# A hybrid decoder layer on one core: the attention query projection moved to the front of the input projections, with the scores of two blocks between their pieces

## The chip, the core and the metric

The kernel runs on one core of a Trainium2 chip. The core has five engines that run side by side and meet through semaphores: TensorE (PE, the matmuls; its weight loads are shown as PEld), VectorE (DVE), ScalarE (ACT), GpSimd (POOL) and SyncE (SP, which here only starts DMA transfers; ACT's queue starts some too). The metric is device time in microseconds (us) of one execution.

## The reference

One decoder layer over 512 tokens of width 1024, in float32. Token mixing: a combined input projection feeds four mLSTM heads and eight sliding-window attention heads, and one output projection takes both. Cross-attention into 256 memory tokens and a retrieval over 16384 experts (PEER) follow; the change does not touch them.

```python
y = rmsnorm(x, g_mix) @ w_in          # mLSTM q, k, v, o gate, i and f gates; attention q, k, v
qk = silu(causal_depthwise_conv(q|k))  # width 4
hm = mlstm_chunkwise(q, k, v, i, f)    # decays exp(log f sums + i), carried state per head
hm = rmsnorm per head(hm) * g_mhead * sigmoid(o)
ha = sliding_window_gqa_sinks(aq, ak, av, sinks)   # window 128: a block sees itself and the block before
x = x + concat(hm, ha) @ w_out
x = x + memory_cross_attention(rmsnorm(x), rmsnorm(mem))
x = x + peer_ffn(rmsnorm(x))
```

## The kernel before, in words

All matmuls keep float32 accuracy with three products: an operand is cut into a high and a low part (`whi`, `wlo` for weights, `xhi`, `xlo` for activations; ACT casts, DVE subtracts; `load_w` L985 and `split_psum` L942), and hi x hi, lo x hi, hi x lo accumulate in PSUM. A projection of 512 columns is two halves of the depth, each with four accumulators (`acc_f` with features in the partitions, `acc_t` with tokens): eight pieces of 12 matmuls each. A weight half is one SP transfer, one cast of 2048 columns and one subtraction, or four of each with 512 columns (`parts=4`).

The front stage, `front()`, makes in this order: the norm of x, the mLSTM values, the small projections (attention k and v, gates), the qk projection with convolution and silu (`evac_qk` L197), the output gate's projection mo with its sigmoid into `gm` (`evac_mo` L214), the decay matrices `ab` (L226) and their sixteen exponentials `dt` (L232), then the attention query projection aq (`evac_aq` L384). Between the pieces of aq a scheduler places, by its own costs and due times, the mLSTM heads' products `st` (L241) with `pt = st * dt` (L244), the carry `wb` (L250) and the first two blocks of `mlstm` (L268).

The tokens stand in four blocks of 128. From there on the order of PE is written out by a table, `MIX` (L62), inside `tc.manual_schedule`: a word is a kind and a block, and each takes one step of a generator. `s` is a block's attention (`swa` L318: scores of the first four heads; scores of the last four and the softmax; transposes of the probabilities, once for block 0 and twice for the others; products with the values), `m` is `mlstm` (numerators; then the state), `n` is `mlstm_out` (normalise, gate, transpose, split), `x` is the output projection's half step for a block (`mix0` L396), `w` loads a half of the output weights.

The orders of ACT, DVE and POOL come from the scheduler, which follows the program with priorities. PSUM has eight banks in three groups by tag: `a`, `b` and `d`. In `swa` of before the scores take banks of `b`.

The reload of `h` (x again, for the residual sums), 4 transfers of 512 KB on SP's queue, and the 8 MB zero fill of a buffer in HBM, on ACT's queue, are issued once the aq projection is through.

Of the kernel before, what the change touches and what calls it, by code (L numbers as in the profile page):

```python
# [11 lines left out]
F32 = mybir.dt.float32  # L12
# [4 lines left out]
AF = mybir.ActivationFunctionType  # L17
ALU = mybir.AluOpType
# [14 lines left out]
NK = 128  # L33
# [7 lines left out]
UG = 4  # L41
# [39 lines left out]
def front(c):  # L81

    tc, nc, a = c.tc, c.nc, c.a
    ident, ps = c.ident, c.ps
    fp = c.fp
# [52 lines left out]
    tp = ps.tile([P, 512], F32, tag="a", name="tp_v")  # L138
    for b in range(NB):
        T.transpose(tp[:, b * P:(b + 1) * P], avT[:, b * P:(b + 1) * P], ident)  # L140
    V.tensor_copy(av, tp.rearrange("p (b d) -> p b d", b=NB))


    t0 = c.np_.tile([P, D], F32, tag="xs", bufs=4, name="rowt0")
# [41 lines left out]
    for b in range(NB):  # L186
        tp = ps.tile([P, 512], F32, tag="a", name="tp_r")
        T.transpose(tp[:, :96], rows[0:96, b * P:(b + 1) * P], ident[:96, :96])
        V.tensor_copy(cols[:, b], tp[:, :96])
# [22 lines left out]
    gm = fp.tile([P, NB, 512], F32, name="gm")  # L212
# [8 lines left out]
    pt, dts = [], []  # L221

    abs_ = [ps.tile([P, 512], F32, tag=t_, name="ab") for t_ in "ddaa"]
    for h in range(4):
        r = slice(32 * h, 32 * h + 4)
        T.matmul(abs_[h], c.sel[r, h], raf4[r], start=True, stop=False)  # L226
    for h in range(4):
        T.matmul(abs_[h], c.identb, c.cmask, start=False, stop=True)
    for h in range(4):
        dt = c.np_.tile([P, D], F32, tag="xs", bufs=4, name="dt")[:, :S]  # L230
        for b in range(NB):
            A.activation(dt[:, b * P:(b + 1) * P], abs_[h][:, b * P:(b + 1) * P], AF.Exp, bias=cols[:, b, h:h + 1])  # L232
        dts.append(dt)
    for pr in range(2):
# [12 lines left out]
    wbs = [ps.tile([P, 512], F32, tag="d", name="wb") for _ in range(2)]
    for pr in (1, 0):
        r = slice(32 * pr, 32 * pr + 4)
        T.matmul(wbs[pr], c.selp[r, pr], wi4[r].rearrange("p b t -> p (b t)"), start=True, stop=True)  # L250
    for pr, wb in enumerate(wbs):
        V.tensor_copy(dec[:, pr], wb.rearrange("p (b t) -> p b t", b=NB)[:, :, P - 1])
        V.tensor_tensor(qk[:, pr], wb, qk[:, pr], op=ALU.mult)
# [63 lines left out]
    def swa(b):  # L317
# [7 lines left out]
        mx = fp.tile([P, 8], F32, tag="mx", bufs=2, name="mx")  # L325
        for jj in range(2):

            sps = [ps.tile([P, 512], F32, tag="b", name="sp") for _ in gs]
            for j2 in range(2):
                for g, r in enumerate(gs):  # L330
                    T.matmul(sps[g][:, j2 * 256:j2 * 256 + nk], aq[r, 2 * jj + j2, t], kT[r, k0:k0 + nk],
                             start=True, stop=True)
            for j2 in range(2):
                for g in range(2):
                    h = 4 * g + 2 * jj + j2
                    V.tensor_tensor_reduce(sc[:, h, :nk], sps[g][:, j2 * 256:j2 * 256 + nk], msk, 1.0, FMIN,
                                           op0=ALU.add, op1=ALU.max, accum_out=mx[:, h:h + 1])
            if jj == 0:
                yield
# [38 lines left out]
    ml = [mlstm(b) for b in range(NB)]  # L378
    for b in range(2):
        step(ml[b], 2)  # L380
    aq = fp.tile([P, 4, S], F32, name="aq")

    def evac_aq(j, acc):
        c.act_aq = A.copy(aq[:, j], acc)  # L384

    gemm_fm(c, [a["w_in_m"][3, hf] for hf in range(2)], evac_aq)

    with tc.issue_after(c.raw_dma.ins):
        for b in range(NB):
            nc.sync.dma_start(c.h[:, b], a["x"][:, b])  # L390
    with tc.issue_after(c.act_aq.ins):
        c.zd = nc.scalar.dma_start(c.wd[0].rearrange("g p n -> p g n"),
                                   zero.unsqueeze(1).to_broadcast([P, NK // UG, P * UG]))
    wo = []

    def mix0(b):  # L396
        acc = ps.tile([P, 512], F32, tag="b", name="acc_o")
        for hf in range(2):
            mm3_tm(c, acc, wo[hf], slice(0, 512), hf, b)
            if hf == 0:  # L400
                yield
        resid(c, b, 0, acc)

    it = {"s": [swa(b) for b in range(NB)], "x": [mix0(b) for b in range(NB)], "m": ml}
    with tc.manual_schedule(engines={mybir.EngineType.PE}):
        for op in MIX.split():
            k, b = op[0], int(op[1])
            if k == "n":
                mlstm_out(b)
            elif k == "w":  # L410
                wo.append(load_w(c, a["w_out"][0, b], 512, parts=4, hp=0 if b else HP))
# [878 lines left out]
```

## Time and profile before

| | |
|---|---|
| median of 3 runs | 1652.22 us (1652.19 to 1653.87) |
| profiled execution | 1653.3 us |
| its span, first to last instruction | 1651.5 us |
| PE busy | 1609.7 us (97%) |
| DVE, ACT, POOL busy | 1235.1 (75%), 723.6 (44%), 591.1 us (36%) |
| mean granted TensorE clock | 0.989 |
| chain that ended last | PE 89%, DVE 4%, DMA 3%, ACT 2% |

The profile is of one execution. A busy share is an average over stages with different limits, so a stage is read from its own rows: the timeline lists each instruction with the idle time of its engine before it and what released it; the waits sum that idle time by line; the windows give busy time and the granted clock of a stretch. [...]

### The profile page before, as it was taken

To read this page: it belongs to the slowest core of one execution; us is meant where nothing else is said; L and a number is where in the kernel's file an instruction comes from. 1 tells how busy PE (TensorE), PEld (TensorE's weight loads), DVE (VectorE), ACT (ScalarE), POOL (GpSimd) and SP (SyncE) were. 2 spreads that over 40 slices of the span, in tenths; PEclk is the share of its full clock that TensorE was granted. 3 is DMA by queue.
4 is the path that set the end of the run, shared out by engine and by line. 5 is a ranking of instruction groups with operands and counts; after the bars stand their busy time and mean duration, and the time that the engine had idled before them with its cause. 6 is when DMAs were issued, how large, how long until landed. Compare 5 with 4: busy or idle time off the path is not lost.

```text
span 1651.5 us, 23090 instructions
## 1 busy us (share of the span) xinstructions
PE 1609.7 (97%) x8388; PEld 1415.1 (86%) x8388; DVE 1235.1 (75%) x2704; ACT 723.6 (44%) x1217; POOL 591.1 (36%) x427
## 2 busy tenths in 40 slices
PE   8998899999999999999999999999999999999994
PEld 5776688878999999999998888888888888888883
DVE  5546564464787887777796888788888888888898
ACT  5445544342544454678664333333333333333332
POOL 2000000000027787877221543444433434334451
PEclk9999999999999999999999999999999999999997
DMA  5236134232254435678999999999989889988895
GB/s 214 77 127 255 59 126 173 77 153 106 96 168 145 116 71 141 181 190 213 342 305 339 410 393 347 343 342 338 334 335 367 338 321 333 362 317 320 323 364 181
DMA packets 151122, 402.17 MB, mean 244 GB/s; under 512 B 28368, under 2 KB 62304, under 8 KB 138848
## 3 DMA queue, kind: packets, MB, share of 16 engines
q1 hardware_dynamic: 58208, 240.04, 39.0%
q0 software_dynamic: 55360, 134.32, 24.8%
q10 hardware_dynamic: 37440, 26.35, 5.1%
q8 instruction: 66, 1.08, 0.3%
q14 instruction: 48, 0.39, 0.1%
HBM read 357.07 MB, written 43.58 MB: 243 GB/s over the span
## 4 chain that ended last, share of the span: by engine, by line
PE 89%; DVE 4%; DMA 3%; ACT 2%; issue 1%; POOL 0%; DVEq 0%; SPq 0%; POOLq 0%; ACTq 0%
PE acc_u L907 10%; PE acc_u L908 10%; PE acc_u L909 10%; PE acc_d L836 10%; PE acc_d L834 10%; PE acc_d L835 10%; PE acc_f L1008 4%; PE acc_f L1009 4%; PE acc_f L1010 4%; PE w L740 3%; DMA wd<-stg 3%; PE acc_t L1023 2%; PE acc_t L1022 2%; PE acc_t L1021 2%; DVE gacc L778 1%
## 5 line engine op out<-in xcount | busy, mean ns | idle before, releaser
L834 PE MATMUL acc_d<-xhi,dh 128*128 128x384 f32 x1024 | 349.8, 342 | 1.0 <-ACT gsp L856 1.0
L836 PE MATMUL acc_d<-xhi,dl 128*128 128x384 f32 x1024 | 345.0, 337 | 1.7 <-DVE dl L823 1.7
L835 PE MATMUL acc_d<-xlo,dh 128*128 128x384 f32 x1024 | 343.6, 336 | 0.0
L908 PE MATMUL acc_u<-ul,ch 128*128 128x512 f32 x762 | 297.7, 391 | 0.0
L909 PE MATMUL acc_u<-uh,cl 128*128 128x512 f32 x762 | 296.6, 391 | 0.0
L685 POOL DMA_INDIRECT wd<-gg,ei x128 | 231.6, 1810 | 147.6 <-DVE ei L679 84.8
L907 PE MATMUL acc_u<-uh,ch 128*128 128x512 f32 x762 | 264.4, 390 | 0.2 <-ACT ch L895 0.2
L762 POOL DMA_INDIRECT rows<-in_up_dram,rowid x128 | 169.4, 1323 | 236.8 <-DVE gacc L778 208.9
L823 DVE TENSOR_TENSOR dl<-draw,dh 128x1024 fp32r<-128x1024 f32 x128 | 156.1, 1220 | 92.8 <-ACT dh L785 90.3
L895 ACT CAST ch<-cf 128x384 fp32r<-128x384 f32 x127 | 65.1, 514 | 356.3 <-issue 339.2
L785 ACT CAST dh<-draw 128x1024 fp32r<-128x1024 f32 x128 | 134.0, 1049 | 195.6 <-PE acc_d L835 170.8
L762 POOL DMA_INDIRECT rows<-in_down_r_dram,rowid x106 | 142.6, 1346 | 199.1 <-DVE dots L768 158.4
L834 PEld LDWEIGHTS acc_d<-xhi,dh 128*128 128x128 f32 x1024 | 192.8, 188 | 5.3 <-ACT gsp L856 1.3
L836 PEld LDWEIGHTS acc_d<-xhi,dl 128*128 128x128 f32 x1024 | 192.6, 188 | 3.9 <-DVE dl L823 2.6
L835 PEld LDWEIGHTS acc_d<-xlo,dh 128*128 128x128 f32 x1024 | 192.8, 188 | 3.7
L909 PEld LDWEIGHTS acc_u<-uh,cl 128*128 128x128 f32 x762 | 143.0, 188 | 29.4
L908 PEld LDWEIGHTS acc_u<-ul,ch 128*128 128x128 f32 x762 | 143.0, 188 | 28.7
L907 PEld LDWEIGHTS acc_u<-uh,ch 128*128 128x128 f32 x762 | 142.9, 188 | 28.3 <-ACT ch L895 0.5
L886 DVE TENSOR_TENSOR ul<-uraw,uh 128x1024 fp32r<-128x1024 f32 x127 | 154.8, 1220 | 12.5 <-ACT uh L785 12.3
L778 DVE SCALAR_TENSOR_TENSOR gacc<-rows,coef,gacc 128x1024 f32<-128x1024 f32 x127 | 162.6, 1280 | 0.9
L768 DVE CUSTOM_DVE_ANT_0 rows<-rows,xn 128x1024 f32<-128x1024 f32 x128 | 153.7, 1218 | 0.0
L896 DVE TENSOR_TENSOR cl<-cf,ch 128x384 fp32r<-128x384 f32 x127 | 70.7, 557 | 86.4 <-ACT ch L895 79.9
(344 smaller groups left out, 2654.0 us busy)
## 6 DMA issues: line engine op xcount, KB each, us to landing
draw<-in_down_t_dram SPq DMA_DIRECT2D x64, 1024.0 KB
uraw<-in_up_dram SPq DMA_DIRECT2D x64, 1024.0 KB
wt<-wd SPq DMA_DIRECT2D x96, 256.0 KB
wd<-stg ACTq DMA_DIRECT2D x8, 2048.0 KB
gd<-gsp SPq DMA_DIRECT2D x18, 768.0 KB
gsr<-gd SPq DMA_DIRECT2D x18, 768.0 KB
wd<-zero ACTq DMA_DIRECT2D x1, 8192.0 KB
raw<-in_w_pq_dram SPq DMA_DIRECT2D x8, 1024.0 KB
```

Source lines behind the costliest of these rows:

```text
L685: i = G.indirect_dma_start(out=out, out_offset=bass.IndirectOffsetOnAxis(ap=ei[:, h, k:k + 1], axis=0), in_=c.gg[:, NG, hh, k:k + 1], in_o ...
L762: G.indirect_dma_start(out=r, out_offset=None, in_=src, in_offset=bass.IndirectOffsetOnAxis(ap=c.rowid[:, j:j + 1], axis=0))
L768: V.tensor_tensor_reduce(r, r, c.xn0, 1.0, 0.0, op0=ALU.mult, op1=ALU.add, accum_out=dots[:, j:j + 1])
L778: V.scalar_tensor_tensor(c.gacc, r, coef[:, j:j + 1], c.gacc, op0=ALU.mult, op1=ALU.add)
L823: c.dl = nc.vector.tensor_tensor(self.lo, raw, f32(self.hi), op=ALU.subtract)
L834: T.matmul(acc[:, :TD], self.hi[:, ks], c.xhi[:, k, NG * P:], start=(k == 0), stop=False)
L835: T.matmul(acc[:, :TD], self.hi[:, ks], c.xlo[:, k, NG * P:], start=False, stop=False)
L836: T.matmul(acc[:, :TD], self.lo[:, ks], c.xhi[:, k, NG * P:], start=False, stop=(k == KT - 1))
L886: V.tensor_tensor(lo, raw, f32(hi), op=ALU.subtract)
L907: T.matmul(acc[b][n], ch[:, t], hi[:, d], start=st, stop=False)
L908: T.matmul(acc[b][n], ch[:, t], lo[:, d], start=False, stop=False)
L909: c.mm = T.matmul(acc[b][n], cl[:, t], hi[:, d], start=False, stop=sp)
```

## The change

The aq projection comes first, then qk, then mo, each as a generator of eight pieces, and `MIX` now writes the order of PE from the first of these pieces on. New words: `a`, `q`, `g` (a piece of aq, qk, mo), `t` and `c` (the transposes of the attention values and of the gate columns), `d` (the decays), `e` (a pair of mLSTM heads), `f` (the carry). The scores of blocks 0 and 1 stand between pieces of qk and use PSUM tag `d`; block 0's transposes stand in mo. `rows` moves to another pool, and `gm`, `aq` and `pt` are allocated ahead. The reload of `h` and the zero fill are issued behind the second half of the output weights.

```diff
-MIX = ("w0 s0 s0 n0 n1 s1 m2 s1 x0 m2 s0 w1 x1 s0 m3 x0 s2 s1 s2 s1 s3 n2 s1 n3 s3 x2 x1 s2 s2 s2 x3 s3 x2 s3 s3 x3")
+MIX = ("a0 a0 a0 t0 a0 a0 a0 a0 a0 c0 q0 s0 q0 q0 s0 q0 q0 s1 q0 q0 s1 q0 g0 g0 d0 g0 g0 w0 e0 g0 e1 s0 g0 f0 m0 g0 m0 g0 w1 "
+       "n0 s0 m1 s2 s1 x0 m1 s1 s2 n1 x0 s1 m2 s3 x1 m2 s2 x1 s3 n2 m3 s2 s2 n3 x2 s3 x2 s3 x3 s3 x3")
...
-    rows = f1.tile([P, S], F32, name="rows")
+    rows = c.np_.tile([P, D], F32, tag="xs", bufs=4, name="rows")[:, :S]
...
     fp = c.fs.enter_context(c.pool("front2"))
+    gm = fp.tile([P, NB, 512], F32, name="gm")
+    aq = fp.tile([P, 4, S], F32, name="aq")
     qk = fp.tile([P, 4, S], F32, name="qk")
...
-    gemm_fm(c, [a["w_in_m"][0, hf] for hf in range(2)], evac_qk)
...
     def evac_mo(b, acc):
-        A.activation(gm[:, b], acc, AF.Sigmoid)
+        c.act_mo = A.activation(gm[:, b], acc, AF.Sigmoid)
         V.tensor_tensor(gm[:, b], gm[:, b], c.gmh, op=ALU.mult)
-    gemm_tm(c, [a["w_in_m"][2, hf] for hf in range(2)], evac_mo)
...
-            sps = [ps.tile([P, 512], F32, tag="b", name="sp") for _ in gs]
+            sps = [ps.tile([P, 512], F32, tag="d" if b < 2 else "b", name="sp") for _ in gs]
...
-    for b in range(2):
-        step(ml[b], 2)
...
-    gemm_fm(c, [a["w_in_m"][3, hf] for hf in range(2)], evac_aq)
-
-    with tc.issue_after(c.raw_dma.ins):
-        for b in range(NB):
-            nc.sync.dma_start(c.h[:, b], a["x"][:, b])
-    with tc.issue_after(c.act_aq.ins):
-        c.zd = nc.scalar.dma_start(c.wd[0].rearrange("g p n -> p g n"),
...
-    it = {"s": [swa(b) for b in range(NB)], "x": [mix0(b) for b in range(NB)], "m": ml}
+    it = {"s": [swa(b) for b in range(NB)], "x": [mix0(b) for b in range(NB)], "m": [mlstm(b) for b in range(NB)],
+          "a": [fm_parts(c, [a["w_in_m"][3, hf] for hf in range(2)], evac_aq)],
+          "q": [fm_parts(c, [a["w_in_m"][0, hf] for hf in range(2)], evac_qk)],
+          "g": [tm_parts(c, [a["w_in_m"][2, hf] for hf in range(2)], evac_mo)]}
+    once = {"t": lambda _: tr_v(), "c": lambda _: tr_c(), "d": lambda _: decays(), "e": heads, "f": lambda _: carry(),
+            "n": mlstm_out,
+            "w": lambda h: wo.append(load_w(c, a["w_out"][0, h], 512, parts=4, hp=0 if h else HP))}
...
+            if op == "w1":
+                with tc.issue_after(c.raw_dma.ins):
+                    for b in range(NB):
+                        nc.sync.dma_start(c.h[:, b], a["x"][:, b])
+                with tc.issue_after(c.act_mo.ins):
+                    c.zd = nc.scalar.dma_start(c.wd[0].rearrange("g p n -> p g n"),
...
+def fm_parts(c, src, evac):
+
+    acc = [c.ps.tile([P, 512], F32, tag="b", name=f"acc_f{j}") for j in range(4)]
+    for hf in range(2):
+        w = load_w(c, src[hf], 512)
+        for j in range(4):
+            mm3_fm(c, acc[j], w, j, hf, S)
+            if hf:
+                evac(j, acc[j])
+            yield
```

`tm_parts` is the same with `acc_t` and `mm3_tm`. `tr_v`, `tr_c`, `decays`, `heads` and `carry` hold the old code of these steps. The changed kernel's line numbers differ from those of before; the rows below carry each kernel's own.

ACT before, from the cast of aq's first half (`whi` 128x2048) past the decays; `acc_t` is the mo projection, `gm` its sigmoid:

```order
L995 CAST whi<-raw 128x2048
L215 ACTIVATE gm<-acc_t_685 128x512
L232 ACT_TABLE_LOAD
L232 ACTIVATE dt<-ab,cols 128x128 x16
L995 CAST whi<-raw 128x512 x4
L384 COPY aq<-acc_f_958 128x512
```

ACT in the change, from the last copy of the qk projection (`convraw`) to the cast of mo's second half; `sc` are the scores of block 1, `qk<-convy` is the silu:

```order
L209 COPY convraw<-acc_f_663 128x512
L357 ACT_TABLE_LOAD
L357 ACTIVATE sc,den_863<-sc,nm 128x256
L355 ACTIVATE es<-es 128x8
L357 ACTIVATE sc,den_863<-sc,nm 128x256 x7
L215 ACT_TABLE_LOAD
L215 ACTIVATE qk<-convy 128x512
L363 ACTIVATE sc<-sc,den_863 128x256 x4
L215 ACTIVATE qk<-convy 128x512
L238 ACT_TABLE_LOAD
L238 ACTIVATE dt<-ab,cols 128x128 x16
L1002 CAST whi<-raw 128x2048
```

The exponentials and scalings of block 1 and two silus, with three table loads, now stand ahead of `dt`, and a cast that PE needs stands behind it.

PE before, in the query projection, around the first pair of heads (`st`); `acc_f` is aq:

```order
L1010 MATMUL acc_f_960<-xhi,wlo 128x512
L241 MATMUL st<-qk 128x128 [waits PE_49,Activation_49]
L241 MATMUL st<-qk 128x128 x2
L241 MATMUL st<-qk 128x128 [waits PE_49,Activation_49]
L241 MATMUL st<-qk 128x128 x4
L1008 MATMUL acc_f_960<-xhi,whi 128x512
```

PE in the change, from the end of mo's fourth piece; `acc_t_904` is the first piece of mo's second half:

```order
L1030 MATMUL acc_t_907<-whi,xlo 128x512
L248 MATMUL st<-qk 128x128 [waits DVE_49,PE_49,Activation_49]
L248 MATMUL st<-qk 128x128 [waits PE_49,Activation_49]
L248 MATMUL st<-qk 128x128 x6
L1028 MATMUL acc_t_904<-whi,xhi 128x512 [waits Activation_49]
L1029 MATMUL acc_t_904<-wlo,xhi 128x512 [waits DVE_49]
L1030 MATMUL acc_t_904<-whi,xlo 128x512
```

The heads now stand between two pieces of mo, directly ahead of the first product that needs mo's second weight half; before, they stood inside aq, whose matmuls went on after them.

ACT before, from the squares of block 3 of the mLSTM (`junk_h`) to the exponentials of block 3's softmax (`den_1487`; `den_1399` is block 2's):

```order
L290 ACTIVATE junk_h,hss<-hm 128x128 x4
L366 COPY pT<-tp_p 128x512 x2
L348 ACTIVATE sc,den_1399<-sc,nm 128x256
L346 ACTIVATE es<-es 128x8
L348 ACTIVATE sc,den_1399<-sc,nm 128x256 x7
L942 CAST xhi<-tp_hm 128x4x128
L942 CAST xhi<-o_att 128x4x128
L942 CAST xhi<-tp_hm 128x4x128
L354 ACTIVATE sc<-sc,den_1399 128x256 x4
L348 ACTIVATE sc,den_1487<-sc,nm 128x256
L346 ACTIVATE es<-es 128x8
L348 ACTIVATE sc,den_1487<-sc,nm 128x256 x7
```

ACT in the change, from the softmax of block 3 (`den_1462`) to the split of block 3's mLSTM heads (`tp_hm`):

```order
L357 ACTIVATE sc,den_1462<-sc,nm 128x256
L355 ACTIVATE es<-es 128x8
L357 ACTIVATE sc,den_1462<-sc,nm 128x256 x7
L293 ACTIVATE den<-num 128x2 x2
L375 COPY pT<-tp_p 128x512
L363 ACTIVATE sc<-sc,den_1462 128x256 x4
L949 CAST xhi<-o_att 128x4x128
L299 ACTIVATE junk_h,hss<-hm 128x128 x4
L949 CAST xhi<-tp_hm 128x4x128
```

The squares of block 3 stood ahead of the softmaxes of blocks 2 and 3, with three splits (`xhi`) between the two; now they stand behind block 3's exponentials, a copy, the scalings and a cast, directly ahead of their split.

## Rows read from the trace of the kernel before

**Rows 1.** PE waits, 230 us to the end: engine, line, releaser: us in total, times, longest.
```profile
PE w L740 <- DVE oh L739: 2.0, 1, 2.0
...
PE acc_u L907 <- ACT ch L895: 0.2, 1, 0.2
```

**Rows 2.** Timeline of PE, 136 to 202 us: start, duration, instruction, [idle before].
```profile
139.63 0.96 PE L298 MATMUL ds<-vx,kw 128*64 128x129 f32 x8 [1.65 <-DVE hm L289]
142.85 1.17 PE L312 MATMUL tp_hm<-ident,hm 128*128 128x128 f32 x4 [1.50 <-DVE hm L310]
...
179.25 0.77 PE L1021 MATMUL acc_o<-whi,xhi 128*128 128x512 f32 x1 [3.21 <-DVE mx L336]
189.36 1.09 PE L363 MATMUL tp_p<-ident,sc 128*128 128x128 f32 x8 [0.68 <-ACT pT L366]
```

**Rows 3.** Windows: PE, PEld, DVE, ACT, POOL busy, granted clock, DMA share, GB/s.
```profile
140.00:148.00 8.00, 6.43 (x33) 4.28 (x31) 6.14 (x28) 6.37 (x29) 1.01 (x1) 0.57 1.04 370
178.00:186.00 8.00, 6.75 (x17) 5.36 (x18) 3.76 (x17) 5.58 (x22) 0.00 (x0) 0.57 0.00 0
```

**Rows 4.** Timeline of PE, 55 to 175 us, single rows.
```profile
55.90 0.40 PE L1008 MATMUL acc_f<-xhi,whi 128*128 128x512 f32 x1
56.13 0.40 PE L1009 MATMUL acc_f<-xlo,whi 128*128 128x512 f32 x1
...
103.49 0.59 PE L1008 MATMUL acc_f<-xhi,whi 128*128 128x512 f32 x1
...
119.33 1.17 PE L241 MATMUL st<-qk 64*128 64x128 f32 x16
...
160.51 0.71 PE L277 MATMUL num<-vx,pt 128*128 128x129 f32 x4
162.64 0.50 PE L1021 MATMUL acc_o<-whi,xhi 128*128 128x512 f32 x1
...
165.65 1.14 PE L331 MATMUL sp<-kT,aq 64*128 64x256 f32 x8
166.71 1.09 PE L363 MATMUL tp_p<-ident,sc 128*128 128x128 f32 x8
...
172.44 1.94 PE L373 MATMUL o_att<-pT,av 128*64 128x512 f32 x8
```

**Rows 5.** Timeline of ACT, 79 to 178 us.
```profile
79.36 1.15 ACT L206 ACTIVATE qk<-convy 128x512 f32<-128x512 f32 x2
...
101.88 1.90 ACT L995 CAST whi<-raw 128x2048 fp32r<-128x2048 f32 x1 [2.26 <-PE acc_t L1023]
...
104.29 1.28 ACT L232 ACT_TABLE_LOAD   x1
105.59 4.23 ACT L232 ACTIVATE dt<-ab,cols 128x128 f32<-128x128 f32 x16
118.97 2.18 ACT L995 CAST whi<-raw 128x512 fp32r<-128x512 f32 x4 [9.15 <-PE acc_f L1009]
...
128.19 0.30 ACT L290 ACTIVATE junk_h<-hm 128x128 f32<-128x128 f32 x1
...
133.04 0.39 ACTq L392 DMA_DIRECT2D wd<-zero  x1
...
177.70 1.71 ACT L354 ACTIVATE sc<-sc,den 128x256 f32<-128x256 f32 x4
```

**Rows 6.** Groups of ACT, 40 to 230 us: count, busy us, mean ns, idle before.
```profile
L348 ACT ACTIVATE sc<-sc,nm 128x256 f32<-128x256 f32 x24 | 11.9, 495 | 5.6 <-DVE nm L342 5.6
```

**Rows 7.** Timeline of DVE, 71 to 168 us.
```profile
71.16 2.29 DVE L996 TENSOR_TENSOR wlo<-raw,whi 128x2048 fp32r<-128x2048 f32 x1 [2.82 <-ACT whi L995]
...
131.42 1.14 DVE L310 SCALAR_TENSOR_TENSOR hm<-hm,rst,gm 128x128 f32<-128x128 f32 x4 [1.14 <-POOL rst L938]
...
167.89 0.42 DVE L336 CUSTOM_DVE_ANT_0 sc<-sp,band 128x256 f32<-128x256 f32 x1
```

**Rows 8.** Timeline of SP's queue, 60 to 240 us.
```profile
192.34 0.80 SPq L436 DMA_DIRECT2D mem<-in_mem_dram  x2
```

More of the change, by code (lines that the diff above doesn't have):

```diff
@@ L185, in front, with tr_c @@
     cols = fp.tile([P, NB, 96], F32, name="cols")
[L186 to L189, printed above, removed]
+    def tr_c():
+        for b in range(NB):
+            tp = ps.tile([P, 512], F32, tag="a", name="tp_r")
+            T.transpose(tp[:, :96], rows[0:96, b * P:(b + 1) * P], ident[:96, :96])
+            V.tensor_copy(cols[:, b], tp[:, :96])
     f1s.close()
     fp = c.fs.enter_context(c.pool("front2"))
+    gm = fp.tile([P, NB, 512], F32, name="gm")
+    aq = fp.tile([P, 4, S], F32, name="aq")
     qk = fp.tile([P, 4, S], F32, name="qk")
@@ L208, in evac_qk, with decays, heads @@
             V.tensor_scalar(qk[:, j], qk[:, j], 0.125, None, op0=ALU.mult)
-    gemm_fm(c, [a["w_in_m"][0, hf] for hf in range(2)], evac_qk)
-    gm = fp.tile([P, NB, 512], F32, name="gm")
     def evac_mo(b, acc):
-        A.activation(gm[:, b], acc, AF.Sigmoid)
+        c.act_mo = A.activation(gm[:, b], acc, AF.Sigmoid)
         V.tensor_tensor(gm[:, b], gm[:, b], c.gmh, op=ALU.mult)
-    gemm_tm(c, [a["w_in_m"][2, hf] for hf in range(2)], evac_mo)
[L221 to L234, printed above, removed]
+    pt = [fp.tile([P, S], F32, name=f"pt{h}") for h in range(4)]
+    dts = []
+    def decays():
+        abs_ = [ps.tile([P, 512], F32, tag=t_, name="ab") for t_ in "ddaa"]
+        for h in range(4):
+            r = slice(32 * h, 32 * h + 4)
+            T.matmul(abs_[h], c.sel[r, h], raf4[r], start=True, stop=False)
+        for h in range(4):
+            T.matmul(abs_[h], c.identb, c.cmask, start=False, stop=True)
+        for h in range(4):
+            dt = c.np_.tile([P, D], F32, tag="xs", bufs=4, name="dt")[:, :S]
+            for b in range(NB):
+                A.activation(dt[:, b * P:(b + 1) * P], abs_[h][:, b * P:(b + 1) * P], AF.Exp, bias=cols[:, b, h:h + 1])
+            dts.append(dt)
+    def heads(pr):
         sts = [ps.tile([P, 512], F32, tag="a", name="st") for _ in range(2)]
@@ L242, in front, with carry @@
         for hh in range(2):
-            pth = fp.tile([P, S], F32, name=f"pt{2 * pr + hh}")
-            V.tensor_tensor(pth, sts[hh], dts[2 * pr + hh], op=ALU.mult)
-            pt.append(pth)
+            V.tensor_tensor(pt[2 * pr + hh], sts[hh], dts[2 * pr + hh], op=ALU.mult)
     dec = fp.tile([P, 2, NB], F32, name="dec")
[L247 to L253, printed above, removed]
+    def carry():
+        wbs = [ps.tile([P, 512], F32, tag="d", name="wb") for _ in range(2)]
+        for pr in (1, 0):
+            r = slice(32 * pr, 32 * pr + 4)
+            T.matmul(wbs[pr], c.selp[r, pr], wi4[r].rearrange("p b t -> p (b t)"), start=True, stop=True)
+        for pr, wb in enumerate(wbs):
+            V.tensor_copy(dec[:, pr], wb.rearrange("p (b t) -> p b t", b=NB)[:, :, P - 1])
+            V.tensor_tensor(qk[:, pr], wb, qk[:, pr], op=ALU.mult)
     def make_kw(b):
@@ L376, in swa @@
             split_psum(c, c.xhi[:, 4:8, t], c.xlo[:, 4:8, t], o.rearrange("p (h t) -> p h t", h=4))
-    ml = [mlstm(b) for b in range(NB)]
-    for b in range(2):
-        step(ml[b], 2)
-    aq = fp.tile([P, 4, S], F32, name="aq")
     def evac_aq(j, acc):
-        c.act_aq = A.copy(aq[:, j], acc)
-    gemm_fm(c, [a["w_in_m"][3, hf] for hf in range(2)], evac_aq)
-    with tc.issue_after(c.raw_dma.ins):
-        for b in range(NB):
-            nc.sync.dma_start(c.h[:, b], a["x"][:, b])
-    with tc.issue_after(c.act_aq.ins):
-        c.zd = nc.scalar.dma_start(c.wd[0].rearrange("g p n -> p g n"),
-                                   zero.unsqueeze(1).to_broadcast([P, NK // UG, P * UG]))
+        A.copy(aq[:, j], acc)
     wo = []
@@ L407, in front @@
             k, b = op[0], int(op[1])
[L408 to L411, printed above, removed]
+            if k in once:
+                once[k](b)
             else:
                 step(it[k][b], 1)
+            if op == "w1":
+                with tc.issue_after(c.raw_dma.ins):
+                    for b in range(NB):
+                        nc.sync.dma_start(c.h[:, b], a["x"][:, b])
+                with tc.issue_after(c.act_mo.ins):
+                    c.zd = nc.scalar.dma_start(c.wd[0].rearrange("g p n -> p g n"),
+                                               zero.unsqueeze(1).to_broadcast([P, NK // UG, P * UG]))
     for k in it.values():
@@ L1041, in gemm_fm, with tm_parts @@
                 evac(j, acc[j])
+def fm_parts(c, src, evac):
[7 more added lines that the diff above has]
+            yield
+def tm_parts(c, src, evac):
+    acc = [c.ps.tile([P, 512], F32, tag="b", name=f"acc_t{j}") for j in range(NB)]
+    for hf in range(2):
+        w = load_w(c, src[hf], 512)
+        for b in range(NB):
+            mm3_tm(c, acc[b], w, slice(0, 512), hf, b)
+            if hf:
+                evac(b, acc[b])
+            yield
 def gemm_tm(c, src, evac, parts=1):
```

7 lines of the change are left out of this document (4 added, 3 removed).

## The prediction

> **What bounds the kernel now.** I read the waits of TensorE (PE) first, over the whole span. From 230 us to the end it waits at seven places, 6.9 us together and nowhere longer than 2.0 [rows 1], and the change orders nothing there anew: whatever the front stage, the first 230 us, gains or loses reaches the end one for one. So the question is only how much PE time the front loses, before and after.
>
> In the front the timeline of PE shows it running without a gap through all input projections and then waiting six times between 137 and 190 us, 8.4 us together; the first, second, fifth and sixth stand in [rows 2] (1.65, 1.50, 3.21, 0.68; the other two are 1.11 and 0.28). [...] **At stake in the old order: 8.4 + 5.7 = 14.1 us.** No matmul is added or removed, so this is the most the change can win.
>
> **The change, part by part.** *Removed.* All six old waits stood behind softmax or mLSTM chains that were squeezed in after the last projection. The new order dissolves each of those places; I count all 14.1 as gained and ask what is late next.
>
> *Place A: decays, heads and the gate projection's second half.* In the old order the decay exponentials (dt) start on ScalarE (ACT) at 105.59 and take 4.23 us [rows 5], while PE has the whole query projection to do; nobody waits. In the new order only two pieces of gate projection lie between the decay matmuls (d0) and the first heads (e0), and ahead of dt stand two softmax blocks and the convolution's silus.
> When is PE at e0? A projection matmul starts every 0.2335 us (55.90 to 56.13), 12 to a piece, 2.80 us. From 55.90 to 103.49 the old PE did 16 pieces, the transposes and the decays [rows 4]. New: those 47.6, four more pieces (11.2), and four steps of scores, 0.7 each for block 0 (half as wide; an estimate from the next) and 1.06 for block 1 (165.65 to 166.71 [rows 4]), 3.5. PE is at e0 at 55.9 + 47.6 + 11.2 + 3.5 = 118.2.
> When is ACT through? The second scores of block 1 end on PE at 55.9 + 15 pieces x 2.80 + 1.0 (transposes, an estimate) + 3.5 = 102.4. ACT then has, by its printed order: four silus 2.3 (two take 1.15), two copies of like size 1.2, four casts 2.18, three table loads 3.84, eight exponentials 4.0 (0.495 each [rows 6]), four scalings 1.71 [rows 5]: 15.2 us. The first silu waits for VectorE (DVE), which has a 2.29 us cut, four row maxima and seven convolution steps ahead of it; that puts it between 102.4 and 104.4, I take 103.4. So dt starts at 118.6. The heads' products need the two banks of dt's heads 2 and 3: 12 of 16 exponentials, 3.2 us, and the last by 122.8. Behind dt, ACT casts the gate projection's second half, 1.90 us, then DVE subtracts, 2.29 [rows 5, 7]: 127.0. PE, after the heads' 1.17 us [rows 4] and one matmul, could have used that at 119.6. **Place A waits 7.4 us**, 6.4 to 8.4 with the bounds of the silu.
>
> *Place B: block 1's mLSTM numerators.* They need the PSUM bank that the first mLSTM transposes hold until they are split. The split stands on ACT behind the last sigmoid 0.6 (a silu's length), four casts of the second output half 2.18, and the issue of the zero fill 0.39 [rows 5], then 0.6 itself, and 0.6 on DVE (a quarter of 2.29): 4.4 us after the last projection piece. PE has some 2.2 us in between (half of eight transposes 0.5, half of eight value products 0.9, two transposes and a numerator, an estimate of 0.8). Bounds: nothing, if the casts find ACT earlier, and 2.8; I take the difference, **2.2**.
>
> *Place C: block 3.* After the second scores of block 3, PE has those scores 1.06, four transposes 0.5, numerators 2.13 (160.51 to 162.64), transposes 1.03, values 1.9 [rows 4], 6.7 us, and then wants block 3's mLSTM result. Its normalisation stands on ACT behind that block's softmax: scores 1.06, maxima 4 x 0.42 less overlap 1.5, three small steps as much as one maximum, 0.4 (an estimate), exponentials 4.0, a copy and a cast of a silu's length 0.6 each, scalings 1.71, then from the first square to the normalised head 128.19 to 131.42, 3.2, and one step 0.3 [rows 5 to 7]: 13.3 us. **Place C waits 6.6**, 5 to 7. In the old order the squares stood ahead of these exponentials.
>
> *Small ones.* The last two old waits were for transposes and scores, 0.68 and 0.28; as much again is likely where block 0's transposes now meet a DVE just given the heads' products: 1.0, between 0 and 2.
>
> *Clock.* After the 1.65 us wait that ended at 139.63 the clock fell, and after the 3.21 us wait too; after the 1.11 us wait it did not [rows 2, 3]. A, B and C are all longer than 1.65, so I take three stretches like the old two. In A about half of the stretch lies in the wait, 1.7; B 3.0 and C 2.7: 7.4 us. Bounds: nothing at all, and three whole ones, 9.0.
> [...] A clock that stays up at B is a case inside the forecast; I give it 0.15 of the forecast's 0.75.
>
> *Moved at no price.* The reload of h (2 MB) moves behind the first output weights on SP's queue and is first added at the first output block, tens of us later. The zero fill of 8 MB leaves ACT at 133.04 in the old order and, behind four more pieces, two pairs of heads and place A's wait, some 17 us later in the new (an estimate); at 370 GB/s [rows 3] it runs 23 us, to about 173, and SP's next load is at 192.34 [rows 8]. That leaves 19 us of cover; without it the load of the memory tokens would share the engines with the fill.
>
> **Sum.** New waits 7.4 + 2.2 + 6.6 + 1.0 = 17.2, new clock 7.4, old 14.1: +10.5 us. On the profiled execution's 1653.3 us that is 1663.8; the median of the runs shown is 1.1 lower, so **1662.7 us, slower by 0.6%**. What a measurement of this kernel can tell from no change is 0.2%, 3.3 us. The terms' bounds don't all fall together; the forecast's own range is +5 to +14.
>
> **The rivals.**
> 1. *ACT keeps ahead* (faster). The projections now cover two softmax blocks, and behind two blocks of softmax the old PE waited only 1.11 and 0.68 us for ACT's transposed copies, so ACT was seldom far behind. If ACT starts dt by 115.0, its cast and DVE's cut are out before 119.6, and block 3's squares are done inside PE's 6.7 us, A and C fall with their clock: 10.5 - 7.4 - 1.7 - 6.6 - 2.7 = -7.9, **1644.3**. Against it: 15.2 us of work queued on ACT, each at a traced length. It decides at whether dt starts before or after PE is at e0. [...]
> 2. *A draw.* Each chain is 2 us shorter (A 5.4, B 0.2, C 4.6, small ones 0) and the clock falls once or twice (1.7 to 4.4): 11.9 to 14.6 against 14.1, **1650 to 1653**.
> 3. *Table switches cost double* (slower still). The three loads in A's queue take 1.28 us each, and dt starts 0.02 us after its load ends [rows 5]: no other price shows. If the engine had also to run empty at each, by as much again, A grows by 3 x 1.28 = 3.8: **1666.5**. [...]
>
> **How the numbers follow.** Forecast 0.75, rival 1 0.10, rival 2 0.09, rival 3 0.06. Slower by over 0.2%: 0.75 + 0.06 = 0.81; same 0.09; faster 0.10. The range leaves out rivals 1 and 2, 0.19 together, and reaches over the forecast's own bounds and rival 3: 1654 to 1667. The price of A carries it, being the longest chain.
>
> **What would show it.** In the changed kernel's PE waits: a wait of 3 to 5 us for ACT's dt at the heads' products near 118 to 123 us, then one of about 3 us on DVE's cut in the gate projection's fifth piece; about 2 us at block 1's numerators; about 5 us at block 3's mLSTM transposes for DVE; three stretches at half clock, one behind each; the first memory key product 10 us later than in the old trace. On ACT no idle time between the second scores and dt. I am wrong if PE goes through e0 without a wait, or if 55 to 230 us hold no more than 14 us of waits and clock loss.

## The result and the profile after

The changed kernel is slower: 1665.57 us in the median (1662.55 to 1666.99, 4 runs) against 1652.2 before, a ratio of 1.008 with a 95% interval of 1.006 to 1.010. The forecast was 1662.7 and the range 1654 to 1667. The profiled execution has a span of 1665.2 us (1651.5 before) at a mean granted clock of 0.986 (0.989); it is the longest of the four (1666.99 us).

The waits of PE in the front of the changed kernel, 55 to 245 us: engine, line, releaser: us in total, times, longest.

```profile
PE tp_hm L321 <- DVE hm L319: 4.4, 1, 4.4
PE num L286 <- DVE xlo L950: 4.4, 2, 2.8
PE st L248 <- ACT dt L238: 3.5, 2, 3.3
PE acc_t L1029 <- DVE wlo L1003: 2.5, 1, 2.5
PE tp_p L372 <- DVE pt L250: 0.9, 1, 0.9
PE num L286 <- DVE qk L261: 0.8, 2, 0.7
PE tp_r L195 <- DVE cols L196: 0.4, 1, 0.4
```

None of the six old waits [rows 2] is in this list (tp_hm here is block 3's, the old one at 142.85 was block 0's), and its sum is 16.9 us instead of 8.4. Place A is the lines st (for dt, 3.5) and acc_t (for the cut of the gate projection's second half, 2.5), place B the longer one of the two num waits for xlo (2.8), place C tp_hm (4.4) with the shorter num wait (1.5) ahead of it. Single rows of place A, from the timelines of ACT, PE and DVE (start, duration, instruction, [idle before]):

```profile
104.53 0.63 ACT L215 ACTIVATE qk<-convy 128x512 f32<-128x512 f32 x1 [2.69 <-DVE convy L214]
...
114.72 1.28 ACT L215 ACT_TABLE_LOAD   x1
116.01 0.63 ACT L215 ACTIVATE qk<-convy 128x512 f32<-128x512 f32 x1
116.55 1.70 ACT L363 ACTIVATE sc<-sc,den 128x256 f32<-128x256 f32 x4
118.15 0.62 ACT L215 ACTIVATE qk<-convy 128x512 f32<-128x512 f32 x1
118.78 1.28 ACT L238 ACT_TABLE_LOAD   x1
120.08 4.23 ACT L238 ACTIVATE dt<-ab,cols 128x128 f32<-128x128 f32 x16
124.09 2.01 ACT L1002 CAST whi<-raw 128x2048 fp32r<-128x2048 f32 x1
```

```profile
119.66 0.39 PE L1030 MATMUL acc_t<-whi,xlo 128*128 128x512 f32 x1
123.33 0.79 PE L248 MATMUL st<-qk 64*128 64x128 f32 x2 [3.29 <-ACT dt L238]
124.36 2.08 PE L248 MATMUL st<-qk 64*128 64x128 f32 x14 [0.24 <-ACT dt L238]
126.37 0.79 PE L1028 MATMUL acc_t<-whi,xhi 128*128 128x512 f32 x1
129.68 0.80 PE L1029 MATMUL acc_t<-wlo,xhi 128*128 128x512 f32 x1 [2.52 <-DVE wlo L1003]
```

```profile
126.14 1.29 DVE L250 TENSOR_TENSOR pt<-st,dt 128x512 f32<-128x512 f32 x2 [8.73 <-ACT whi L1002]
127.34 2.28 DVE L1003 TENSOR_TENSOR wlo<-raw,whi 128x2048 fp32r<-128x2048 f32 x1
```

ACT has no gap from 114.72 to 126: a table load, two silus with block 1's scalings between them, the next load, dt from 120.08, the cast. PE arrives behind the matmul of 119.66 and stands still until dt's third head is done, and after the heads it stands again until DVE has cut what ACT casts at 124.09; DVE makes the heads' products `pt` first.

Places B and C, from the timelines of ACT and PE:

```profile
154.32 0.58 ACT L949 CAST xhi<-tp_hm 128x512 fp32r<-128x512 f32 x1
```

```profile
156.57 0.46 PE L286 MATMUL num<-vx,pt 128*128 128x129 f32 x2 [2.81 <-DVE xlo L950]
...
198.82 1.17 PE L321 MATMUL tp_hm<-ident,hm 128*128 128x128 f32 x4 [4.45 <-DVE hm L319]
```

The clock, in four windows of the changed kernel (busy time of PE, PEld, DVE, ACT, POOL; granted clock as a share of full speed; DMA share; GB/s):

```profile
122.00:134.00 12.00, 7.91 (x30) 5.81 (x30) 3.49 (x3) 5.38 (x11) 0.00 (x0) 0.57 0.25 82
142.00:148.00 6.00, 5.65 (x20) 4.41 (x20) 2.92 (x13) 1.96 (x10) 0.92 (x1) 0.72 0.01 4
156.00:164.00 8.00, 7.43 (x33) 5.92 (x34) 4.16 (x20) 2.44 (x11) 1.01 (x1) 0.57 1.03 361
196.00:206.00 10.00, 7.18 (x26) 5.83 (x27) 2.66 (x8) 1.63 (x8) 1.01 (x1) 0.66 0.17 61
```

By the sum of length x (1 - clock) these lose 5.2, 1.7, 3.4 and 3.4 us, 13.7 together. PE was idle for 3.3 us of the slow part of the first and 0.9 of the last; half of that comes off, since the clock there is 0.50, so an estimated **11.6 us** are on the path. Place A's stretch is 10 us long (0.50 in each whole us from 123 to 133), not 7, and holds two waits; and there is a fourth, from 143.3 (0.50 from 144 to 146), behind waits of 0.92, 0.66 and 0.18 us. In the kernel before the same reckoning gives 5.7: its two windows of 8 us at 0.57 [rows 3] lose 3.4 us each, less half of the 1.50 and 0.8 us in which PE was idle there, 2.7 and 3.0. Inside them the clock is at half:

```profile
144.00:146.00 2.00, 2.00 (x10) 1.18 (x9) 1.46 (x6) 1.94 (x8) 0.00 (x0) 0.50 1.05 400
...
182.00:184.00 2.00, 2.00 (x6) 1.59 (x5) 0.00 (x0) 2.00 (x10) 0.00 (x0) 0.50 0.00 0
```

What reaches the rest of the kernel is the start of the first memory key product, here in the timelines of PE of the kernel before and of the changed kernel:

```profile
229.15 0.28 PE L1008 MATMUL acc_mk<-mhi,whi 128*128 128x256 f32 x1
```

```profile
241.23 0.28 PE L1015 MATMUL acc_mk<-mhi,whi 128*128 128x256 f32 x1
```

It comes 12.1 us later, 0.3 of it because the projections start later in this execution (56.17 instead of 55.90). Waits give +8.5, the clock +5.9; what is left, -2.6, is PE work that became shorter: from the first of these projections to this row PE is busy for 164.8 us before and for 168.1 after; less the clock's loss that is 159.1 and 156.5 for the same matmuls. In the old order the scheduler had put the heads, the carry and numerators between matmuls of the query projection, and such a switch shows there as a matmul that takes 0.42 us (103.49 [rows 4] to 103.91) instead of 0.2335. That this is the whole 2.6 is an inference; no run tries it. Behind 245 us PE waits 8.5 us in this execution (6.9 before [rows 1]), 2.1 of it in one place of the expert stage that shows 0.2 to 1.2 in other executions. That makes up the 13.7 us between the two spans.

### The profile page after: what moved, and what is told of

Read it like the earlier page. It is cut to its first block, busy times and chain, and to the rows that moved or that the text cites. A ratio compares the mean times of both kernels' runs of the same rounds, so it can differ in the third digit from the quotient of the medians.

```text
span 1665.2 us, 23092 instructions
## 1 busy us (share of the span) xinstructions
PE 1614.1 (97%) x8388; PEld 1417.9 (85%) x8388; DVE 1234.1 (74%) x2704; ACT 727.1 (44%) x1220; POOL 590.0 (35%) x427
## 4 chain that ended last, share of the span: by engine, by line
PE 89%; DVE 3%; DMA 3%; ACT 3%; issue 1%; POOL 0%; DVEq 0%; SPq 0%; POOLq 0%; ACTq 0%
PE acc_u L914 10%; PE acc_u L915 10%; PE acc_u L916 10%; PE acc_d L843 10%; PE acc_d L841 10%; PE acc_d L842 10%; PE acc_f L1015 4%; PE acc_f L1016 4%; PE acc_f L1017 4%; PE w L747 3%; DMA wd<-stg 3%; PE acc_t L1029 2%; PE acc_t L1030 2%; PE acc_t L1028 2%; PE s L587 1%
## 5 line engine op out<-in xcount | busy, mean ns | idle before, releaser
L914 PEld LDWEIGHTS acc_u<-uh,ch 128*128 128x128 f32 x762 | 143.3, 188 | 30.4 <-ACT ch L902 2.4
```

The source lines that it names most:

```text
L914: T.matmul(acc[b][n], ch[:, t], hi[:, d], start=st, stop=False)
```

## Experiments

All are measured against runs of the kernel before on the same chip (its medians there: 1653.3, 1654.3 and 1653.1), so the ratio to it is what is compared. The changed kernel has 1.0080 by the first result and 1.0069 by the first run below. Gains over it are given below as differences of medians, which cross chips; by the ratios they are 6.0 to 7.8 us for e1_n3_late, 3.5 to 5.3 for e6_m1_late, 4.3 to 6.1 for e2_w0_late, 9.6 to 11.4 for e5_fill and 16.2 to 18.0 for e8_three_moves. The table of PE's order is `MIX`; where one is edited, only the words around the move are shown.

**The changed kernel again, on the chip of the last group.**

> The changed kernel as it is, on one chip with the two others, to set its distance from the kernel before and from its repairs on the same chip. By the first result 1.008 of the kernel before, with waits of 16.9 us after 55 us in its front; a rival of chance (that its first runs met a slow chip) gives 1.004 or less.

1665.38 us, ratio 1.0069 (1.0054 to 1.0084), waits of 16.8 us in the front in the same seven places, and the same four slow stretches. The loss is the kernel's and not a chip's.

**Place C alone.**

```diff
-... n2 m3 s2 s2 n3 x2 s3 x2 s3 x3 s3 x3
+... n2 m3 s2 s2 x2 s3 x2 n3 s3 x3 s3 x3
```

> The changed kernel with one step of PE's table moved: block 3's mLSTM transposes (n3) go behind both half steps of block 2's output projection and one score step, so 6.7 us more of PE work lie ahead of them. Theory (place C is a wait of its own, 4.45 us in the changed kernel's trace, with a half-clock stretch of some 3.0 us behind it): the wait and the stretch go, 1665.6 - 7.4 = about 1658, 1656 to 1661. Rival (PE is bound by ACT's and DVE's total work there, so the wait only moves to the next consumer): within 1.5 us of the changed kernel, with a wait of 4 us elsewhere after 185 us.

1658.07 us, ratio 1.0033 (1.0023 to 1.0043), 7.5 us below the changed kernel, as the theory had it. The wait for hm is gone, 0.5 us appears at the product that needs the split, and no slice from 166 to 212 us is slow (a clock of 1.00 in each).

**Place B alone.**

```diff
-... w1 n0 s0 m1 s2 s1 x0 m1 s1 ...
+... w1 n0 s0 s2 s1 m1 x0 m1 s1 ...
```

> The changed kernel with block 1's numerators (m1) moved in the table behind a score step of block 2 and a transpose step of block 1, so 2.1 us more of PE work lie ahead of them. Theory (place B is a wait of its own for the bank that the first mLSTM transposes hold, 2.81 us, with a half-clock stretch of 3.4 us behind it): most of the wait goes, 1 us at most reappears at the transposes' consumer, and the clock stays up: 4 to 6 us faster than the changed kernel, 1660 to 1662. Rival (the wait only moves to the steps that were brought forward): within 1.5 us.

1660.04 us, ratio 1.0048 (1.0035 to 1.0060), 5.5 us less. The 2.8 us wait is gone, 1.0 reappears at block 1's numerators and 0.7 at its transposes for ACT's copy; the stretch from 157 us is gone (1.00 from 148 to 194 us). So B's price was mostly clock: by the sum used above this kernel loses 8.5 us to it, 5.2 less than the changed kernel, part of that by a shorter stretch behind place C.

**Place A, the second half: is the cast late because ACT is full?**

```diff
-... g0 g0 d0 g0 g0 w0 e0 g0 e1 s0 ...
+... g0 g0 d0 g0 g0 e0 g0 w0 e1 s0 ...
```

> The changed kernel with the load of the output weights' first half (w0) moved in the table behind the fifth piece of the gate projection, whose step loads that projection's second weight half. Theory new after the result (the cast of the gate projection's second half stands behind dt because w0 took the weight buffer that the query-key projection set free, and the next buffer is free only at the end of the gate projection's fourth piece): the cast moves ahead of dt, the wait of 2.52 us for DVE's cut goes, the wait for dt stays near 3.5 us; 1.3 to 2.5 us faster than the changed kernel, about 1663.5. Rival (the prediction's: the cast is late because ACT's queue is full, so what is taken from behind dt is added ahead of it): the wait for dt grows by 1.5 to 2 us and the time stays within 1 us.

1659.30 us, ratio 1.0043 (1.0030 to 1.0056). ACT's and PE's timelines of this kernel:

```profile
106.91 1.91 ACT L1002 CAST whi<-raw 128x2048 fp32r<-128x2048 f32 x1
...
120.14 4.23 ACT L238 ACTIVATE dt<-ab,cols 128x128 f32<-128x128 f32 x16
124.15 2.28 ACT L1002 CAST whi<-raw 128x512 fp32r<-128x512 f32 x4
```

```profile
123.39 0.62 PE L248 MATMUL st<-qk 64*128 64x128 f32 x2 [3.01 <-ACT dt L238]
124.42 2.07 PE L248 MATMUL st<-qk 64*128 64x128 f32 x14 [0.41 <-ACT dt L238]
126.42 0.79 PE L1028 MATMUL acc_t<-whi,xhi 128*128 128x512 f32 x1
127.01 0.63 PE L1029 MATMUL acc_t<-wlo,xhi 128*128 128x512 f32 x1
```

The gate projection's second cast now runs at 106.91, the four casts of the output weights stand behind dt in its place, dt starts at 120.14 as before (120.08), and the wait for the cut is gone while that for dt stays. So it was not first of all ACT's length that held this cast, as the prediction had it, but the weight buffer: `load_w` has two, and `w0` stood ahead of the second gate half in the program and took the one that was free. The other came free when PE was through the gate projection's fourth piece, at 120.05 in the changed kernel; only the last 4.0 us, to 124.09, did the cast stand behind dt. The gain, 6.3 us, is larger than the 2.5 us wait, by the ratios too; in the profile the other part is the clock, whose stretches are five here (0.57 to 0.72 in their windows) but lose 10.2 us by the same sum, 3.5 less than in the changed kernel. I had expected the clock not to move.

**Place A, the first half: is dt late because of ACT's queue?** On the kernel of the last experiment:

```diff
-... s1 q0 q0 s1 q0 g0 g0 d0 g0 g0 e0 g0 w0 e1 s0 g0 f0 ...
+... s1 q0 q0 q0 g0 g0 d0 g0 g0 e0 g0 w0 e1 s0 g0 s1 f0 ...
```

> The kernel of e2_w0_late with block 1's second scores and softmax moved in the table from between the last query-key pieces to behind the second pair of heads, so that its eight exponentials, four scalings and a table load leave ACT's queue ahead of dt. Theory (place A's wait for dt is the length of ACT's queue): the wait of 3.4 us for dt falls to 1.5 or less, and with it that place's half-clock stretch; 3 to 5 us faster than e2_w0_late, 1654 to 1656, less up to 3 us for new waits where the softmax now stands. Rival (ACT is late for another reason, the silus' convolutions on DVE): the wait for dt stays above 3 us and the time is that of e2_w0_late or slower.

1654.57 us, ratio 1.0004 (0.9991 to 1.0017), 4.7 us below e2_w0_late by the medians and 6.4 by the ratios. From ACT's timeline and the waits of PE of this kernel:

```profile
114.02 0.63 ACT L215 ACTIVATE qk<-convy 128x512 f32<-128x512 f32 x1 [2.53 <-DVE convy L214]
114.67 1.28 ACT L238 ACT_TABLE_LOAD   x1
115.96 4.23 ACT L238 ACTIVATE dt<-ab,cols 128x128 f32<-128x128 f32 x16
```

```profile
PE wb L258 <- DVE mx L345: 1.0, 1, 1.0
PE st L248 <- ACT dt L238: 0.8, 2, 0.5
```

Without block 1's softmax ahead of it dt starts 4.2 us earlier, the wait for it falls from 3.4 to 0.8 us, and the new place of the softmax costs 1.0 at the carry. It starts no earlier than that because the last silu now waits 2.5 us for DVE's convolution: there the DVE chain is the next limit, and the rival is right for that rest.

**The clock alone.** Part of PE's waits is filled with products on constants that nobody reads; what PE waits for is meant to come as late as before. In e11_before_fill, below, 14 such products take 3.19 us, 0.23 each. The edit adds to the loop over `MIX`:

```diff
+    FILL = {"e0": [10], "g0": [0, 0, 0, 0, 8], "m1": [11], "n3": [18]}
+    FTAG = {"e0": "d", "g0": "d", "m1": "a", "n3": "a"}
...
+            for _ in range(FILL.get(op, [0]).pop(0) if FILL.get(op) else 0):
+                if _ == 0:
+                    warm = ps.tile([P, 512], F32, tag=FTAG[op], name="warm")
+                T.matmul(warm, c.identb, c.cmask, start=True, stop=True)
```

> The changed kernel with 47 extra bf16 matmuls of 512 columns on constants, into banks that are free, at the three places: 10 ahead of the first heads (e0), 8 ahead of the gate projection's fifth piece, 11 ahead of block 1's numerators, 18 ahead of block 3's mLSTM transposes; about 0.21 us each, so they fit inside the waits of 3.3, 2.5, 2.8 and 4.45 us. Nothing that is waited for comes earlier. Theory (the granted clock falls because of the waits, and the half-clock stretches behind A, B and C cost some 3 us each on the path): three or four of the four stretches go, 7 to 11 us faster than the changed kernel, 1655 to 1659, with the same waits less the filled part. Rival (the clock falls for another reason, or slow PE time is hidden by the chains that PE waits for anyway): 0 to 2 us faster, or slower by what the fill overshoots.

1654.89 us, ratio 1.0011 (1.0002 to 1.0020): 10.7 us faster than the changed kernel with 47 matmuls more. The same windows in this kernel, and the one that is slow:

```profile
122.00:134.00 12.00, 9.82 (x64) 6.14 (x63) 5.19 (x6) 6.29 (x14) 0.00 (x0) 1.00 0.29 100
142.00:148.00 6.00, 6.00 (x34) 4.54 (x32) 3.49 (x13) 2.38 (x10) 1.02 (x1) 1.00 0.01 1
156.00:164.00 8.00, 8.00 (x50) 6.10 (x50) 6.69 (x30) 3.84 (x10) 1.01 (x1) 1.00 1.04 392
182.00:188.00 6.00, 6.00 (x27) 3.30 (x28) 3.36 (x15) 5.87 (x22) 0.00 (x0) 0.72 0.01 3
```

Three of the changed kernel's four windows are at full clock, and the fourth stretch is gone from its place too (1.00 from 188 to 212 us); one of 3.4 us has appeared at 182. One producer did not stay as late as it was, as DVE's timeline of this kernel shows:

```profile
126.44 2.29 DVE L1009 TENSOR_TENSOR wlo<-raw,whi 128x2048 fp32r<-128x2048 f32 x1 [8.74 <-ACT whi L1008]
128.65 1.28 DVE L250 TENSOR_TENSOR pt<-st,dt 128x512 f32<-128x512 f32 x2
```

The cut now stands ahead of the heads' products and ends 1.2 us earlier, counted from the first matmul of the projections (56.45 here, 56.17 in the changed kernel), so about that much of the 10.7 us is not the clock's. The rest is: over all executions the mean granted clock is 0.984 to 0.988 in nine of the changed kernel and 0.990 to 0.994 in the 11 of this one, by span x (1 - clock) some 11 us less. At the places that were filled the slow stretches are therefore a cost of their own, largely on the path: with PE busy in part of the waits the clock there is 1.00 instead of 0.57 and 0.66.

**Three moves together.** e1_n3_late, e6_m1_late and e2_w0_late in one table.

> The moves of e1_n3_late, e2_w0_late and e6_m1_late together. Theory (the three places are separate and their waits and slow stretches add): 7.5 + 6.3 + 5.5 = 19.3 us faster than the changed kernel's 1665.6, about 1646 and faster than the kernel before (1652 to 1653); the one big wait left is that for dt, 3.4 us, with one stretch. Rival (the moves partly gain the same thing, since a place reached earlier finds ACT and DVE later): half of it, 1655 to 1657, with waits of over 2 us grown where single moves had none.

1649.87 us, ratio 0.9971 (0.9958 to 0.9984): **faster than the kernel before**, and 15.7 us below the changed kernel, four fifths of the sum of the single gains by the medians. By the ratios it is 16.2 to 18.0 of 13.8 to 19.2, so that the three places add within the noise. The largest waits of PE in its front:

```profile
PE st L248 <- ACT dt L238: 3.3, 2, 3.0
PE num L286 <- DVE xlo L950: 2.5, 2, 1.5
PE tp_p L372 <- DVE pt L250: 0.9, 1, 0.9
```

**Heads later.**

```diff
-... d0 g0 g0 e0 g0 w0 e1 s0 g0 f0 m0 g0 m0 g0 w1 ...
+... d0 g0 g0 g0 w0 e0 g0 s0 e1 g0 f0 m0 m0 g0 w1 ...
```

> The kernel of e8_three_moves with the first heads (e0) moved behind the sixth piece of the gate projection and the second (e1) behind the seventh, so that four pieces instead of two lie between the decays and the first heads. Theory (cover between dt's exponentials and their consumer is what the order before had and the change took away): the wait for dt falls from 3.4 us to about 1 and its stretch goes, against some 2 us of new waits at the mLSTM steps that move closer together: 2 to 4 us faster than e8_three_moves, 1642 to 1645. Rival (the mLSTM chain behind the heads is the longer one): the same time as e8_three_moves or slower, with waits of over 3 us at block 0's numerators or state.

The wait for dt falls from 3.3 to 0.8 us, 1.3 appears at block 0's state, and in the profile the first memory key product comes at 225.43 instead of 227.97. But the 12 runs have a median of 1649.42 (1646.4 to 1654.4) and a ratio of 0.9980 (0.9967 to 0.9993): not to be told from e8_three_moves. The profile is of the fastest of the 12. That cover takes away the wait is shown by the trace, a gain is not.

**The one wait left, filled.** e8_three_moves with `FILL = {"e0": [10]}`.

> The kernel of e8_three_moves with 10 extra bf16 matmuls of 512 columns on constants ahead of the first heads, inside the one big wait that is left (3.3 us for dt). Theory (the wait itself stays, only the half-clock stretch from 122.7 to 130 us, some 3.3 us, goes): 3 us faster than e8_three_moves, ratio to the kernel before 0.995. Rival (after the moves the slow time is covered): the ratio of e8_three_moves, 0.997.

No slice between 110 and 212 us is slow in this kernel's profile (1.00 in each), and the memory key product comes at 224.82, 3.2 us earlier (3.9 counted from the first matmul of the projections); yet the ratio is 0.9976 (0.9964 to 0.9987), no better than e8_three_moves. The chip is another than e8_three_moves had, and the ratio carries 0.1% on either side; still, the 3 us that the theory took from one execution do not show, though the two intervals do not rule them out. Open.

**The same in the kernel before.** `FILL = {"x2": [14]}` in its table's loop.

> The kernel before, with 14 extra bf16 matmuls of 512 columns on constants ahead of the first half step of block 2's output projection, inside the old wait of 3.21 us that ends at 179.25. Theory (the half-clock stretch behind that wait costs 3.0 us, as the prediction priced it): the stretch from 178 to 185 us goes, 3 us faster than the kernel before, ratio about 0.998. Rival (the slow stretch is hidden, or comes anyway): no difference, ratio 0.9995 to 1.0015.

Windows of this kernel at the place of [rows 3]:

```profile
140.00:148.00 8.00, 5.99 (x30) 4.04 (x30) 6.14 (x26) 6.96 (x31) 1.01 (x1) 0.65 1.04 370
178.00:186.00 8.00, 7.91 (x35) 5.43 (x34) 4.30 (x18) 6.11 (x22) 0.00 (x0) 1.00 0.01 2
```

The second stretch is gone from the profile (1.00 instead of 0.57), but 1652.35 us and a ratio of 0.9998 (0.9987 to 1.0010) hold at most 2.1 us of the 3.0 expected. The profile is of the fastest of its 11 executions, so it shows more than their mean. The runs of the kernel before suggest why one profile misprices this: on the chip of the first group 19 of 20 executions went from 1649.4 us at a mean clock of 0.992 to 1655.5 at 0.986 (the other took 5351 us). If its slow stretches are not the same in every execution, taking away the one that a profile showed takes away only a part of their mean. That is not the whole of it: over all executions the mean clock is 0.9914 here and 0.9900 in the 18 of the kernel before on this chip, some 2 us less slow clock, and the time is still the same. So a stretch that a profile shows is not always paid in full; why not here, no run shows.

**Is it the interleaving or the early query projection?**

```diff
-... c0 q0 s0 q0 q0 s0 q0 q0 s1 q0 q0 s1 q0 g0 g0 d0 g0 g0 w0 e0 g0 e1 s0 g0 f0 m0 g0 m0 g0 w1 n0 ...
+... c0 q0 q0 q0 q0 q0 q0 q0 q0 g0 g0 d0 g0 g0 w0 e0 g0 e1 s0 g0 s0 f0 m0 g0 s1 m0 g0 s1 w1 s0 n0 ...
```

> The changed kernel with the query projection still first but no scores between the pieces of the query-key projection: both blocks' scores and softmax go behind the heads, among the gate projection's last pieces. It tells whether the interleaving or the early query projection costs the time. Theory (what hurts is the missing cover behind dt and the late steps, and the interleaving itself is worth something): dt is early and place A is down to the wait for the weights' cut, but both softmax blocks are now squeezed behind the projections: slower than the changed kernel, 1668 to 1674, with new waits of over 3 us between 140 and 165 us. Rival (the softmax ahead of dt is the loss of the change): faster than the changed kernel by 4 us or more.

1663.90 us, ratio 1.0061 (1.0044 to 1.0078): neither slower nor faster than the changed kernel (1.0069, 1.0054 to 1.0084). Both forecasts were wrong. The first four waits of PE in its front:

```profile
PE tp_hm L321 <- DVE hm L319: 4.4, 1, 4.4
PE tp_p L372 <- DVE sc L365: 3.4, 1, 3.4
PE ds L307 <- DVE mx L345: 3.3, 2, 3.0
PE acc_t L1029 <- DVE wlo L1003: 2.3, 1, 2.3
```

The wait for dt is gone, as the theory had it, and new waits of 3.0 and 3.4 us for the softmax stand in its place. The interleaving paid its price at place A and earned it back behind the projections: in these two placements it is worth nothing. The loss against the kernel before is there without it, so it comes with the early query projection and the places of the steps behind it, not with the scores between the pieces.

## Why the prediction was right, and where it was off

*The frame held.* Behind 245 us nothing changed but 1.6 us in one execution; the delay of the first memory key product is 12.1 of the 13.7 us of span. All six old waits went, as counted. The terms fell less well than the sum, as the next lines show.

*Place A*, 7.4 predicted, 3.5 + 2.5 = 6.0 measured. dt starts at 120.08 instead of 118.6, and PE is at e0 at 119.9 instead of 118.2: the first silu came at 104.53, just past its bounds (102.4 to 104.4), and the switches between projection and scores had been left out of PE's side. That the two errors cancel is luck. Two more steps were left out: DVE made the heads' products ahead of the cut (126.14 and 127.34), 1.2 us more to wait, and PE's own work there, the heads and one matmul, took 3.6 us at a clock of 0.50 instead of 1.4, 2.2 us less to wait. e7_s1_late confirms the reason for the first wait (ACT's queue, with block 1's softmax in it). The reason for the second was wrong: the step "behind dt, ACT casts the gate projection's second half" took the queue's order for the cause, and e2_w0_late shows that it was the buffer up to 120.05 and dt only for the last 4.0 us.

*Place B*, 2.2 predicted, 2.8 measured, with the cast where it was expected (154.32, behind the output weights' four); removing it gave 5.5 with its stretch, 5.2 by the prediction (2.2 + 3.0).

*Place C*, 6.6 predicted (its terms as listed add up to 6.7), 4.45 + 1.54 = 6.0 measured in its two waits; e1_n3_late took back 7.5 us, which the sum of the wait at the transposes and its stretch explains (4.4 + 3.0).

*Small ones*, 1.0 predicted, 2.1 measured (tp_p 0.9, num 0.8, tp_r 0.4), just over the bound of 2. Waits in all: 17.2 against 16.9; the four misses, -1.4, +0.6, -0.6 and +1.1, cancel by luck.

*Clock*, 7.4 predicted, 11.6 measured: **the term that was mis-sized**. I took three stretches like the old two. Place A's is half as long again: it holds two waits, and with the second one gone (e2_w0_late) the clock is 0.66 from 122 to 132 us, 7 us of half clock (0.50 from 124 to 130) instead of 10. A fourth came where the longest wait was 0.92 us. e5_fill shows that most of it is paid on the path: 10.7 us came back, about 1.2 of them by the earlier cut. The case in which the clock stays up at B did not come: in the window from 156 to 164 us it is 0.57, behind a wait of 2.8 us, and it is 0.72 in the one from 142 to 148 us, behind waits of at most 0.92 us. The 5.7 us of the old order, and with them the 3.0 and 2.7 taken for B and C, no run shows as time on the path: they are an estimate from the two windows of [rows 3], and e11_before_fill, in whose profile the second of these is at 1.00, gained at most 2.1 us of its 3.0.

*Left out*: the 2.6 us by which PE's own work became shorter, of the other sign (by fewer switches, an inference, as said above), and the 0.3 us of the later start. Together: 17.2 - 8.4 + 7.4 - 5.7 = 10.5 forecast, 16.9 - 8.4 + 11.6 - 5.7 - 2.6 + 0.3 = 12.1 in the front. That the forecast came so near is luck in part: more than half of the clock's miss of 4.2 us was taken back by a term that had been left out.

*The rivals.* ACT keeps ahead (1644.3): no, dt started after PE was at e0; but its sign was right, since e8_three_moves and e9_heads_late, which give ACT and DVE the lead at these places, came to 1649.9 and 1649.4, some 5 us above its price; in the first, place A's wait for dt is still there. Table switches cost double (1666.5): the time is near this rival's, but not for its reason. The three loads ahead of dt take 1.28 us each, and each next instruction starts 0.01 to 0.02 us behind (109.26 and 110.55, 114.72 and 116.01, 118.78 and 120.08): no price beyond the load shows. Three loads are 3.8 us of the queue that PE waited for.

*Moved at no price*, right: the zero fill leaves ACT at 151.77, 18.7 us later, and its traffic is over by 178, ahead of SP's next load at 193.36.

## What to carry to other kernels

A stage whose exponentials are covered by a long projection behind them loses that cover when the projection is moved ahead (here PE then waited 3.5 us for dt); before such a move, write down for each chain on ACT and DVE what PE has to do until it needs the result, in the new order, and keep those two numbers apart in the table. A wait of PE is priced with the slow stretch behind it, which in the changed kernel's profile cost two thirds as much again as the waits (an estimated 11.6 us beside 16.9), though not every stretch that one profile shows is paid (the fill of the kernel before has a ratio of 0.9998). A late cast is looked up in two places, the queue and the buffer it needs. Filling a wait with throw-away matmuls is a way to tell the two costs apart (10.7 us in e5_fill), if one looks whether the fill moved anything else, and a step moved by a few words is a cheap way to take both.

## What was not expected of the hardware

The four slow stretches of the changed kernel's profile are 10, 3.4, 7 and 7 us long. The longest holds two waits; the wait for dt alone had 7 us behind it in e2_w0_late. The shortest began behind waits of 0.92, 0.66 and 0.18 us, while PE ran the small products of block 0's numerators. What brought the clock down there is not shown: in e5_fill the same three waits stand, and the clock stays at 1.00 from 142 to 148 us. From execution to execution the mean clock changes: the kernel before went from 1649.4 us at 0.992 to 1655.5 at 0.986, so a profile's clock term is good to some 3 us, an estimate, half of that difference.
